# Pseudo-random factors on the ranks of a scan's weave, early splits of two inputs, and head sums by four column tiles

## The chip, the core and the metric

The kernel runs on one core of a Trainium2 chip, in one launch. The time is device microseconds of one execution on the chip; lower is better. Before the change the median of three runs was 1632.7 us (1623.32 to 1636.57).

An engine executes its own instructions strictly in the order in which they were written into its program. TensorE is called PE here (PEld is its loading of stationary operands), VectorE DVE, ScalarE ACT, GpSimd POOL, SyncE SP. SP and POOL issue the transfers between the core's memory and DRAM.

## The reference, cut to what matters

Two requests, each of 512 tokens by 1024 channels, go through two layers with shared weights. Layer 0 is a bidirectional RWKV-7 mixer, layer 1 a neighbourhood attention on a grid. All is float32.

```python
x_prev = jnp.pad(xn[:, :-1], ((0, 0), (1, 0), (0, 0)))
x_next = jnp.pad(xn[:, 1:], ((0, 0), (0, 1), (0, 0)))
xx = 0.5 * (x_prev + x_next) - xn
lerp = lambda j: xn + xx * mu[j]
r = heads(lerp(0) @ w_r).astype(f32)
k = heads(lerp(1) @ w_k).astype(f32)
v = heads(lerp(2) @ w_v).astype(f32)
z = xn @ w_z
kk = k * k_k.astype(f32).reshape(N_HEADS, HEAD_DIM)
kk = kk / jnp.maximum(jnp.sqrt(jnp.sum(kk * kk, axis=-1, keepdims=True)), 1e-12)
...
def step(s, inp):                       # one token of the WKV scan
    r_t, w_t, k_t, v_t, a_t, b_t = inp
    sa = jnp.einsum('bhvk,bhk->bhv', s, a_t)
    s = s * w_t[:, :, None, :] + sa[..., None] * b_t[:, :, None, :] + v_t[..., None] * k_t[:, :, None, :]
    return s, jnp.einsum('bhvk,bhk->bhv', s, r_t)
...
ys.append(_wkv7_scan(r, decay, k_d, v, -kk, kk * a, reverse=(d == 1)))   # d = 0, 1; 16 heads of 64
...
out = y.reshape(bsz, t, D_INNER).astype(xn.dtype) * jax.nn.silu(z)
return out @ w_o
```

Layer 1 multiplies by `w_in` (q, k, v and gate), attends to an 8 by 16 window, gates, and multiplies by `w_ao`. RMS norms stand around both layers.

## The kernel before, in words

**Tiles.** Activations lie with channels on the 128 partitions: eight tiles of 128 by 512 (k = 0 to 7). A product by a weight column (128 output channels) takes eight k-steps. For precision each operand is split into a rounded float32r half and a rest: ACT casts the high half, DVE subtracts (L403 and L404, `halves`; in the scan L806 and L808 for weights, L832 and L834 for inputs). A k-step is three matmuls of 128x512: high by high, high by low, low by high (L454 to L456 in `gemm`, L887 to L889 in the scan). Weight halves live in four pairs of buffers (`whi`, `wlo`, NW = 4), two pairs to a column. Input halves live in 18 buffers (`act`).

**Stage 1, the prelude** (`run`, `prelude`, `columns`, `column`). PE multiplies request 0 by `w_z` (8 columns), by the first LoRA factors, then by `w_k` (8 columns). Beside it DVE and ACT normalise both requests, form the shifted sums `xx`, and mix them with the inputs by a learned factor (`lerp`: ACT scales, L675, DVE multiplies and adds, L676). The mixed inputs of request 1, and that for v of request 0, go to DRAM by way of four `ls` buffers (`mixed`, 32 of them). Those for k and r of request 0 are mixed into `xr` and split into `act` buffers by `shifted`: the ones for k where the z columns end, the ones for r after the k columns have been written. In this stage a list scheduler sets each engine's order, from priorities in the order of the code and its own estimates of durations.

**Head sums.** After each k column `column` copies it out (L717), squares it (L726, tile `tmp`), sums the squares over the 64 channels of each of its two heads by one plain float32 matmul with a stationary operand of two columns (L730, profiled as two instructions), copies the 2x512 result (L733) and stores it to DRAM. When the eighth is there, 16 rows are loaded, a square root (L744) and a reciprocal (L747) are taken, and the result `rn` is stored. `prep`, below, loads it.

**Stage 2, the scan** (`scan_phase`, `weave`). Here a planner of the kernel writes the order of PE, DVE and ACT. Work is cut into threads. Each names the engine of its next piece and when that may start by the planner's clock; of those that may start now, all that are not for PE come ahead of those for PE, and then the lowest rank wins. Ranks are: the 64 scan steps 0; the factors of the next step 0.5 and 1 (`alone`, `near`, `outer`); `preps` 1.5; posts of a product column 2; `merges` 2.4; splits of inputs 2.5; splits of weights 3 or 9; `finish` 4; `inverse` 5; the products 9. A split that the products will soon lack gets 1.2. The products (`flow`) are the remaining columns of both requests' layer 0 (r, v, k, z, the output), and most of layer 1's input columns for request 0: 84 columns, 672 k-steps. Where the planner finds nothing to do on PE for 300 ns and its clock window not full, it writes a filler matmul into spare room (L1730) which computes nothing that is used.

The scan runs in 8 groups of 8 steps (2 requests by 4 sets of 4 heads). Before a group stand `prep` (L977 to L1070: decays, keys and so on, with a round trip of `ab` through DRAM), an elimination on DVE (`elimination`, a chain of 60 instructions L1096 and L1098 between two transposes, L1089 and L1109) and `merges`.

**Stage 3, the rest** (`rest`): what remains of layer 1 for request 0, attention, and request 1's output and layer 1, again in the list scheduler's order.

## Time and profile before

| | |
|---|---|
| median of 3 runs | 1632.7 us (1623.32, 1632.70, 1636.57) |
| the profiled execution | 1627.51 us, of which its span is 1625.7 us |
| busy in the span | PE 1533.0 us (94%), DVE 1219.6 (75%), ACT 974.4 (60%), POOL 199.4 (12%) |
| mean granted TensorE clock | 0.978 |
| chain that ended last | PE 71%, DVE 10%, DMA 8%, ACT 5%, issue 5% |
| prelude | PE from 8.8 us to 154.4 us |
| scan, first to last step | 253.1 us to 1101 us |
| last product of the scan stage | 1143 us |

The span is what the profiled execution took from its first instruction to its last. A row of the timeline has the start, the time that it covers, engine, line, operation, output tile from input tiles, shape and count, and, in brackets, how long the engine sat idle before it and what ended that. Matmuls overlap: a 128x512 matmul is shown as about 390 ns, while its neighbours start some 230 ns apart, and it is the distance of the starts that counts. In a table of windows the granted clock (PEclk) is a share of full speed.

### The profile page before, as it was taken

The page shows a single profiled execution, that of the slowest core. Times are in us where ns is not written, and L with a number is a line of the kernel's source. Part 1 is how long each engine was busy: PE and PEld are TensorE (multiplying, and loading weights), DVE is VectorE, ACT ScalarE, POOL GpSimd, SP SyncE. Part 2 cuts the span into 40 slices and gives each one's busy share as a digit, 9 for nine tenths or more (in the row PEclk, how much of TensorE's full clock was granted, in tenths as well). Part 3 has the DMA queues.
Part 4 walks back from the last instruction along what each step waited for, and adds up shares of the span by engine and source line. Part 5 has one row for each costly group of instructions (what it writes and reads, how often), then busy time and mean ns, then how long its engine had stood idle before and what let it go on. Part 6 is the DMA issues. An engine that isn't in the chain of part 4 may idle for free.

```text
span 1625.7 us, 46321 instructions
## 1 busy us (share of the span) xinstructions
PE 1533.0 (94%) x18700; PEld 1177.7 (72%) x18700; DVE 1219.6 (75%) x2714; ACT 974.4 (60%) x1933; POOL 199.4 (12%) x368
## 2 busy tenths in 40 slices
PE   7989998899989998988999999999999999999998
PEld 6856776666667776766777777777777788777776
DVE  8986587689878788885899999656667585664664
ACT  6567565756647456656676655544567665464562
POOL 0001123301111012122000011000110002110110
PEclk9989999999999999998999999999999999999999
DMA  6447687766676867678776785565766356655553
GB/s 242 158 164 260 217 277 233 261 203 224 196 235 202 261 233 225 207 234 261 234 261 232 253 259 170 160 200 196 258 213 184 115 151 225 225 187 192 170 168 110
DMA packets 183542, 343.61 MB, mean 211 GB/s; under 512 B 25856, under 2 KB 58752, under 8 KB 183328
## 3 DMA queue, kind: packets, MB, share of 16 engines
q1 hardware_dynamic: 158144, 256.75, 49.4%
q0 software_dynamic: 25184, 83.90, 14.7%
q8 instruction: 147, 2.41, 0.6%
q14 instruction: 67, 0.55, 0.1%
HBM read 230.33 MB, written 107.09 MB: 208 GB/s over the span
## 4 chain that ended last, share of the span: by engine, by line
PE 71%; DVE 10%; DMA 8%; ACT 5%; issue 5%; SPq 0%; DVEq 0%; POOL 0%; ACTq 0%; POOLq 0%
PE pm L887 8%; PE pg L456 7%; PE pm L888 6%; PE pm L889 6%; PE pg L454 6%; PE pg L455 6%; PE pf L1199 3%; PE sc L1538 2%; DMA dab<-ab 2%; PE po L1571 2%; PE pt L1556 2%; PE us L1318 2%; PE zy L1271 2%; PE us L1298 2%; PE zy L1322 2%
## 5 line engine op out<-in xcount | busy, mean ns | idle before, releaser
L887 PE MATMUL pm<-act,whi 128*128 128x512 f32 x672 | 297.0, 442 | 2.4 <-ACT NA L1141 1.2
L888 PE MATMUL pm<-act,whi 128*128 128x512 f32 x672 | 269.4, 401 | 7.1 <-DVE act L834 7.0
L889 PE MATMUL pm<-act,wlo 128*128 128x512 f32 x672 | 268.5, 400 | 6.3 <-DVE wlo L808 6.3
L887 PEld LDWEIGHTS pm<-act,whi 128*128 128x128 f32 x672 | 128.9, 192 | 45.4 <-issue 12.9
L454 PE MATMUL pg<-act,whi 128*128 128x512 f32 x384 | 157.7, 411 | 0.0
L889 PEld LDWEIGHTS pm<-act,wlo 128*128 128x128 f32 x672 | 128.9, 192 | 37.0 <-DVE wlo L808 8.3
L888 PEld LDWEIGHTS pm<-act,whi 128*128 128x128 f32 x672 | 129.5, 193 | 33.6 <-DVE act L834 12.1
L456 PE MATMUL pg<-act,wlo 128*128 128x512 f32 x384 | 153.0, 398 | 0.0
L455 PE MATMUL pg<-act,whi 128*128 128x512 f32 x384 | 152.5, 398 | 0.0
L404 DVE TENSOR_TENSOR wlo<-raw,whi 128x512 fp32r<-128x512 f32 x148 | 101.7, 689 | 67.7 <-ACT whi L403 62.2
L403 ACT CAST whi<-raw 128x512 fp32r<-128x512 f32 x148 | 91.2, 617 | 94.2 <-PE pg L455 64.0
L808 DVE TENSOR_TENSOR wlo<-raw,whi 128x512 fp32r<-128x512 f32 x168 | 114.7, 684 | 30.2 <-ACT whi L806 30.1
L806 ACT CAST whi<-raw 128x512 fp32r<-128x512 f32 x168 | 103.7, 620 | 42.0 <-PE pm L888 34.8
L456 PEld LDWEIGHTS pg<-act,wlo 128*128 128x128 f32 x384 | 72.3, 188 | 18.0 <-issue 4.0
L1098 DVE TENSOR_TENSOR N<-etmp,N 128x30 f32<-128x30 f32 (+14 forms) x240 | 78.8, 328 | 4.6
L1096 DVE TENSOR_TENSOR etmp<-N 128x30 f32<-128x30 f32 (+14 forms) x240 | 78.7, 328 | 4.6
L455 PEld LDWEIGHTS pg<-act,whi 128*128 128x128 f32 x384 | 72.5, 189 | 13.1 <-issue 1.3
L454 PEld LDWEIGHTS pg<-act,whi 128*128 128x128 f32 x384 | 72.3, 189 | 12.1 <-issue 0.7
L1552 ACT ACTIVATE sb<-sb,mx 128x256 f32<-128x256 f32 x128 | 64.2, 503 | 23.7 <-DVE mx L1551 22.9
L1199 PE MATMUL pf<-cab 64*64 64x128 f32 (+1 forms) x2048 | 67.6, 268 | 5.6 <-issue 5.2
L1310 ACT COPY X<-us 64x256 f32<-64x256 f32 x128 | 46.9, 366 | 34.4 <-PE zy L1177 32.8
L1222 DVE TENSOR_TENSOR AK<-zy,cc 128x256 f32<-128x256 f32 x63 | 26.6, 423 | 51.7 <-PE zy L1177 49.5
(393 smaller groups left out, 3552.1 us busy)
## 6 DMA issues: line engine op xcount, KB each, us to landing
dab<-ab POOLq DMA_DIRECT2D x32, 1024.0 KB, 7.2
cab<-dab SPq DMA_DIRECT2D x64, 512.0 KB, 4.5
raw<-in_w_in_dram SPq DMA_DIRECT2D x128, 256.0 KB, 3.9
bias<-in_rpb_dram SPq DMA_DIRECT2D x32, 384.0 KB, 4.7
raw<-in_w_z_dram SPq DMA_DIRECT2D x32, 256.0 KB, 4.3
raw<-in_w_k_dram SPq DMA_DIRECT2D x32, 256.0 KB, 2.4
raw<-in_w_r_dram SPq DMA_DIRECT2D x32, 256.0 KB, 4.4
k<-dk SPq DMA_DIRECT2D x32, 256.0 KB, 4.0
```

The lines of the kernel that those rows point to most:

```text
L403: self.nc.scalar.copy(hi, src)
L404: (eng or self.nc.vector).tensor_tensor(lo, src, hi.bitcast(F32), op=ALU.subtract)
L454: nc.tensor.matmul(ps, hi, x[k][0], start=(k == 0), stop=False)
L455: nc.tensor.matmul(ps, hi, x[k][1], start=False, stop=False)
L456: self.mm = nc.tensor.matmul(ps, lo, x[k][0], start=False, stop=(k == KT - 1))
L806: nc.scalar.copy(hi, raw[h])
L808: nc.vector.tensor_tensor(lo, raw.pop(h), hi.bitcast(F32), op=ALU.subtract)
L887: nc.tensor.matmul(ps, hi[:, at], xh, start=(k == 0), stop=False)
L888: nc.tensor.matmul(ps, hi[:, at], xl, start=False, stop=False)
L889: nc.tensor.matmul(ps, lo[:, at], xh, start=False, stop=(k == KT - 1))
L1098: vt.tensor_tensor(N[:, q + 1:, :q], tv, N[:, q + 1:, :q], op=ALU.add)
L1199: end = nc.tensor.matmul(st.f[half(a), h, 0, d, g] if st.last else st.f[half(a), h, :, d, g], ab[half(h), d, g, 2 * e[d] + 1 - a], rt if s ...
```

## The change

It has six parts.

1. **Factors on ranks.** In `weave` a rank is multiplied by `1 + 0.4 u`, with u drawn evenly from -1 to 1 anew for each candidate each time. The generator is seeded anew whenever the number of finished steps passes a multiple of four, from a table of 17 seeds. Five of them are 0, and there ranks stay as they were (segments 1, 7 and 14 to 16).
2. **k inputs early.** `prelude(0)` mixes and splits request 0's inputs for k right after the LoRA matmuls have been written, into the 16 buffers `lw` that held LoRA weights.
3. **r inputs early.** A generator `ahead`, advanced at a quarter of the rate of the k columns, mixes and splits the inputs for r, and loads and splits both halves of the first `w_r` column. These hold two of the four weight buffers until the scan's first product.
4. **Head sums by four tiles.** The matmul of 2x512 becomes four, each of 32 stationary columns (16 copies of either head's selector, with the value 0.5, which the scale 2.0 in the square root makes good) on 128 tokens, to partitions 0, 32, 64 and 96. The copy is 128x128 instead of 2x512, and eight of its rows go to DRAM. The planner's cost for a 128x32 tile is changed with it.
5. **Head sums later.** A k column's sum is not written with its column but after the fourth k-step of the next. The last one becomes a thread of the weave (`tail`, rank 0).
6. **Order in the prelude.** Request 1's norm waits 14 more turns (`HOLD`); request 0's mixed v goes from the end of `prelude(0)` into `prelude(1)`, each with a wait on the latest matmul written.

```diff
-        elif ts == (128, 128):
+        elif ts in ((128, 128), (128, 32)):
             c = max(1.73 * n + 1, 100.0)
...
+    RATE, HOLD = 0.25, 14
+    SEEDS, SIG, SEG = (653160, 0, 317010, 943442, 878710, 392232, 801855, 0, 390308, 625245, 854555, 218764, 664198, 404737, 0, 0, 0), 0.4, 4
...
-        self.ident, self.bones, self.ssel = c("ident", 128), c("bones", 128), c("ssel", 2)
+        self.ident, self.bones, self.ssel = c("ident", 128), c("bones", 128), self.cc[:, CC["bones"] + 48:CC["bones"] + 80]
...
+        for _ in range(s * self.HOLD):
+            yield
         rstd = self.rstd(acc, (lambda: self.mm) if s else None)
...
         if s:
             for k in range(KT):
+                self.mixed(0, "v", 2, k, self.mm)
+                yield
+            for k in range(KT):
                 for kind, j in (("k", 1), ("r", 0), ("v", 2)):
...
+        for k in range(KT):
+            hi, lo = (self.t("lw", (P, 4, 2, 64), 16, F32R, self.lp).rearrange("p k q c -> p (k q c)") for _ in range(2))
+            t = self.t("xr", bufs=self.NXR)
+            self.lerp(t, xn[k], xx[k], 8 + k)
+            self.xk.append(self.halves(t, lo, hi))
+            yield
...
+    def ahead(self):
+
+        xn, xx = self.shift[0]
         for k in range(KT):
-            mixed("v", 2, k)
+            lo, hi = self.pair()
+            t = self.t("xr", bufs=self.NXR)
+            self.lerp(t, xn[k], xx[k], k)
+            self.xr.append(self.halves(t, hi, lo))
+            yield
+        for raw in self.raws(self.a["w_r"][0]):
+            hi, lo = (self.t(tag, (P, self.WP), self.NW, F32R) for tag in ("whi", "wlo"))
+            self.wr.append(self.halves(raw, lo, hi))
             yield
...
-            ss = self.p("pm", (2, T))
-            nc.tensor.matmul(ss, self.ssel, sq, start=True, stop=True)
+            ss = self.p("pm", (P, P))
+            for j in range(4):
+                nc.tensor.matmul(ss[32 * j:32 * j + 32], self.ssel, sq[:, j * P:(j + 1) * P], start=True, stop=True)
             yield "A"
-            row = self.tmp((2, T))
+            row = self.tmp((P, P))
             act.copy(row, ss)
...
-            self.load(sp["ss", s][2 * p:2 * p + 2], row)
+            self.load(sp["ss", s][2 * p:2 * p + 2].rearrange("a (j t) -> j a t", j=4), row[0:P:16])
...
-                act.activation(rn, rn, AF.Sqrt)
+                act.activation(rn, rn, AF.Sqrt, scale=2.0)
...
     def columns(self, s, kind, x, ps=range(NP)):
+        self.tail = None
         for p in ps:
             w = self.first.pop() if self.first else self.weight(self.a["w_" + kind][p])
-            ps = yield from self.gemm(w, x, self.gt)
-            for _ in self.column(s, kind, p, ps):
-                pass
+            gemm, n = self.gemm(w, x, self.gt), 0
+            while True:
...
+                n += 1
+                if n == 4 and self.tail:
+                    run(self.tail[1])
+                    self.tail = None
+                yield
+            end = self.column(s, kind, p, out)
+            if kind == "k":
+                for _ in range(3):
+                    at = next(end)
+                self.tail = at, end
+            else:
+                run(end)
             yield
...
+            if did["steps"] // self.SEG != part:
+                part = did["steps"] // self.SEG
+                dice = Random(self.SEEDS[part])
...
-                    key = (t.eng == "P", t.rank())
+                    key = (t.eng == "P", t.rank() * (1.0 + self.SIG * dice.uniform(-1.0, 1.0) if self.SEEDS[part] else 1.0))
...
+        def tail():
+            (eng, gate, needs), end = self.tail
+            yield eng, gate, lambda c: max(needs(c), 2500.0)
+            yield from end
...
-        run(self.columns(0, "k", self.shifted(0, 1)), (a, 1))
+        run(self.columns(0, "k", self.xk), (a, 1), (self.ahead(), self.RATE))
         run(a)
-        self.xr = self.shifted(0, 0)
```

What this does to the order is shown at three places. A row has the line, the operation, the output tile from the input tiles with their buffer numbers, and the shape. The rows of the kernel after have its own line numbers: L457 to L459 are L454 to L456 of before, L485 is L482, L499 is L496, L759 is L730, L937 to L939 are L887 to L889, L1784 is L1730, L1184 is L1134.

PE at request 1's norm, before: `acc` is the sum of request 1's squares, `pm` the norm's banks, `zy_979` the first k column.

```order
L456 MATMUL zy_979<-act_936,wlo_972 128x512
L454 MATMUL zy_979<-act_943,whi_975 128x512
L482 MATMUL pm_865<-ones,acc_782 128x1 x4
L455 MATMUL zy_979<-act_942,whi_975 128x512
L456 MATMUL zy_979<-act_943,wlo_976 128x512
```

PE at the same norm, after: `zy_1064` is the third k column, `zy_1144` the fourth, `tmp_951` and `tmp_1042` the squares of the first and second.

```order
L459 MATMUL zy_1064<-lw_706,wlo_1061 128x512
L485 MATMUL pm_976<-ones,acc_798 128x1 x4
L499 MATMUL pm_989<-tmp_984,ones 128x128
L759 MATMUL pm_1006<-tmp_951,cc 32x128 x4
L499 MATMUL pm_989<-tmp_984,ones 128x128 x3
L759 MATMUL pm_1082<-tmp_1042,cc 32x128 x4
L457 MATMUL zy_1144<-lw_616,whi_1136 128x512
```

The norm has moved from the middle of the first k column to behind the third. Its second half (L499) follows its first (L485) directly, where eight rows of products stood between the two before, and two head sums stand there too.

PE where the prelude ends and the products of the scan begin, before: `zy_1471` is the last k column, `zy_1594` the filler's bank, `pm_1618` the first r column.

```order
L456 MATMUL zy_1471<-act_964,wlo_1468 128x512
L730 MATMUL pm_1454<-tmp_1452,cc 2x512
L730 MATMUL pm_1502<-tmp_1500,cc 2x512
L1730 MATMUL zy_1594<-cc 128x256 x6
L887 MATMUL pm_1618<-act_1518,whi_1609 128x512
```

PE at the same place, after: `zy_1545` is the last k column, `pm_1622` the first r column, `tmp_1526` the squares of the seventh k column.

```order
L459 MATMUL zy_1545<-lw_706,wlo_1542 128x512
L759 MATMUL pm_1565<-tmp_1526,cc 32x128 x4
L937 MATMUL pm_1622<-act_928,whi_1291 128x512
L938 MATMUL pm_1622<-act_929,whi_1291 128x512
L939 MATMUL pm_1622<-act_928,wlo_1292 128x512
L937 MATMUL pm_1622<-act_953,whi_1291 128x512
L938 MATMUL pm_1622<-act_954,whi_1291 128x512
L939 MATMUL pm_1622<-act_953,wlo_1292 128x512
```

The sum that is left there is the seventh. The last one (`pm_1640`) has moved from ahead of the first r column to behind its twelfth matmul, and the six fillers are gone.

ACT in the last k columns, before: `ls` are mixed inputs on their way to DRAM, `whi` weight halves, `xr` and `act` the inputs for r, of which the last four are made after the last column's square (L726).

```order
L726 ACTIVATE tmp_1500<-zy_1471,cv 128x512
L403 CAST act_1546<-xr_1542 128x512
L675 ACTIVATE xr_1556<-xn_131,dv 128x512
L403 CAST act_1553<-xr_1549 128x512
L733 COPY tmp_1504<-pm_1502 2x512
```

ACT at the same place, after: `pm_1640` is the last column's head sum, L754 is L726, L762 is L733, L701 is L675, L856 is L806.

```order
L754 ACTIVATE tmp_1589<-zy_1545,cv 128x512
L701 ACTIVATE ls_1391<-xn_788,dv 128x512
L701 ACTIVATE ls_1399<-xn_788,dv 128x512
L762 COPY tmp_1654<-pm_1640 128x128
L856 CAST whi_1666<-raw_1635 128x512
```

The inputs for r are gone from there, and the mixed inputs of request 1 have moved behind: the last 14 of the 32 now stand behind the last k column's square, among the splits for the r columns, where none stood before.

In the whole weave, the rows of L1730 add up to 62 fillers before and those of L1784 to 42 after. The rows from the first attention scores to the end of the program are nearly the same in both.

33 lines of the change are left out of this document (24 added, 9 removed).

## The prediction

> **What bounds the kernel now.** I read the page first, then a table of windows by stage, then PE's timeline where it stops, then the groups for prices. The page's busy times:
>
> ```profile
> PE 1533.0 (94%) x18700; PEld 1177.7 (72%) x18700; DVE 1219.6 (75%) x2714; ACT 974.4 (60%) x1933; POOL 199.4 (12%) x368
> ```
>
> PE is busy nearly all the time, so what can be won is PE's idle time, its slow clock, fillers, and matmuls that become cheaper. The windows by stage (columns: window, length, busy us and count of PE, PEld, DVE, ACT, POOL, granted clock, DMA share, GB/s) say where these are. The cuts are PE's first wait in the first k column, the first r product, the first scan step, the fourth group's start, the last step and the last product:
>
> ```profile
> 0.00:82.00 82.00, 72.94 (x315) 59.19 (x316) 72.23 (x155) 52.65 (x87) 1.53 (x40) 1.00 0.58 200
> 82.00:154.00 72.00, 61.91 (x225) 41.50 (x224) 57.42 (x94) 54.73 (x96) 3.67 (x3) 0.88 0.59 210
> 154.00:253.00 99.00, 91.55 (x736) 71.47 (x734) 68.60 (x123) 56.85 (x109) 20.57 (x35) 0.98 0.74 247
> 253.00:605.00 352.00, 324.73 (x5736) 240.96 (x5737) 282.69 (x553) 213.67 (x419) 52.48 (x88) 0.96 0.70 224
> 605.00:1101.00 496.00, 464.42 (x8762) 356.61 (x8765) 406.30 (x797) 302.85 (x574) 66.35 (x107) 0.98 0.69 225
> 1101.00:1143.00 42.00, 42.00 (x248) 33.25 (x239) 25.67 (x54) 20.21 (x36) 3.24 (x6) 1.00 0.67 231
> 1143.00:1626.00 483.00, 475.46 (x2699) 374.67 (x2697) 306.68 (x945) 273.46 (x614) 51.54 (x89) 1.00 0.56 181
> ```
>
> From 1101 us on PE is busy at full clock, and nothing of the change is there: whatever is won before shifts all of it. The k columns (82 to 154 us) are the worst stage: 10 us idle and a clock of 0.88. In the scan PE is idle for 27 us and then 32 us, and the clock, 4% and 2% short, costs some 14 us and 10 us more. There DVE is busy 80% and 82%. PE's timeline in the k columns names the waits:
>
> ```profile
> 83.57 0.51 PE L454 MATMUL zy<-act,whi 128*128 128x512 f32 x1 [1.00 <-ACT act L403]
> 87.14 1.84 PE L482 MATMUL pm<-ones,acc 128*128 128x1 f32 x8 [3.06 <-DVE acc L469]
> 102.78 1.87 PE L730 MATMUL pm<-tmp,cc 128*2 128x512 f32 x2 [2.44 <-ACT tmp L726]
> 148.39 1.86 PE L730 MATMUL pm<-tmp,cc 128*2 128x512 f32 x2 [3.48 <-ACT tmp L726]
> 150.18 4.55 PE L1730 MATMUL zy<-cc 128*128 128x256 f32 x12
> 154.38 0.59 PE L887 MATMUL pm<-act,whi 128*128 128x512 f32 x1
> ```
>
> PE waits for the first split input, for the norm's sum, twice for a square, and then six fillers (two instructions each) pass until the first r inputs are split. The clock falls behind each of these:
>
> ```profile
> 80.00:90.00 10.00, 5.94 (x24) 4.68 (x23) 10.00 (x18) 6.57 (x12) 0.00 (x0) 0.77 0.31 105
> 90.00:100.00 10.00, 9.89 (x42) 7.58 (x40) 8.93 (x19) 9.91 (x17) 0.00 (x0) 0.89 0.18 66
> 100.00:110.00 10.00, 7.55 (x22) 3.65 (x21) 10.00 (x18) 5.25 (x10) 0.00 (x0) 0.83 0.66 251
> 140.00:150.00 10.00, 6.52 (x22) 3.13 (x20) 7.85 (x12) 9.98 (x19) 1.85 (x2) 0.84 0.60 225
> 150.00:160.00 10.00, 10.00 (x37) 8.10 (x37) 5.67 (x12) 6.30 (x13) 0.00 (x0) 0.82 0.67 186
> ```
>
> **The change part by part.** *Early k and r inputs, later sums, the moved norm.* By the order all four waits lose their cause: k inputs are split before the k columns, the norm stands two columns later, most sums wait for squares that are half a column old or more, and r inputs and the first r weights are ready when the last k column ends. Idle time removed: 1.00 + 3.06 + 2.44 + 3.48 = 10.0 us. The fillers are gone too: 154.38 - 150.18 = 4.2 us. The slow clock in the five slices is 10 x (0.23 + 0.11 + 0.17 + 0.16 + 0.18) = 8.5 us; 14 of those 50 us were idle or fillers, so the share on products is about 6 us.
>
> Against it stand new waits. Behind the third k column the norm's two halves follow each other directly, with ACT and DVE work between them, and at the fifth column a sum stands three rows behind the end of its own column, on a square that ACT reaches only after two mixed inputs that wait for stores. The nearest row for either is the 2.44 us above, so 4.9 us; at best 0, at worst 3.48 each and a third one, 10. The row of slice 100 to 110 shows that a wait of 2.44 us already took the clock to 0.83 there, so I add 1.7 us once. By the Trainium skill (TensorE: Matmul & The Clock Gate, "What's actually happening") the clock falls after an idle window of about 3.4 us. This trace differs: 2.44 us sufficed. By the page's figure the 1.7 us would not come.
>
> *The price of a head sum.* In an undisturbed place a sum costs what it pushes its neighbours apart:
>
> ```profile
> 136.96 0.39 PE L456 MATMUL zy<-act,wlo 128*128 128x512 f32 x1
> 137.28 1.02 PE L730 MATMUL pm<-tmp,cc 128*2 128x512 f32 x2
> 138.23 0.50 PE L454 MATMUL zy<-act,whi 128*128 128x512 f32 x1
> ...
> 229.45 0.39 PE L889 MATMUL pm<-act,wlo 128*128 128x512 f32 x1
> 229.68 1.03 PE L764 MATMUL pm<-cc,tmp 128*128 128x128 f32 x8
> 230.52 0.50 PE L887 MATMUL pm<-act,whi 128*128 128x512 f32 x1
> ...
> 1157.24 1.09 PE L1571 MATMUL po<-pts,vtok 128*64 128x128 f32 x16
> 1158.27 1.13 PE L1538 MATMUL sc<-k,q 64*128 64x256 f32 x6
> ```
>
> The distance is 1.27 us, less the 0.23 us of a product's own: 1.04 us. Eight full-width instructions of 128 take 0.84 us (229.68 to 230.52), as many columns as a sum's two of 512, so 0.2 us of a sum is the change of tile form. Four tiles are again eight instructions of 128. Two column tiles that alternate take 1.03 / 16 = 0.064 us each, against 0.84 / 8 = 0.105: they run side by side. By that row eight instructions take 0.51 us, were all four side by side 0.21; were they one after the other, 0.84. With the 0.2 us a sum then costs 0.4 to 1.04 us. I take 0.55, between the first two: 0.5 us less. Eight in the prelude give 4 us (0 to 5), eight in the scan 4 us.
>
> The Trainium skill has a rule against this (TensorEngine Tiling (Array Packing), "Key Properties"): a change of tiling mode drains the engine. The trace bears a price out, the 0.2 us, but the sum of before pays it as well, so it does not speak between the two.
>
> *The copy of a sum* is a quarter as long. ACT spends 0.571 us on it now:
>
> ```profile
> L733 ACT COPY tmp<-pm 2x512 f32<-2x512 f32 x16 | 9.1, 571 | 14.5 <-PE pm L730 14.4
> ```
>
> Some 0.35 us by 16 is 6 us of ACT work, at 60% busy: hidden by PE's products, counted at nothing. A store of eight short rows instead of two long ones also has nobody waiting but at the last sum.
>
> *What of the prelude's lead survives.* The first r product comes earlier by 10.0 + 4.2 + 6 + 4 - 4.9 - 1.7 = 17.6 us, near 137 us. But the scan begins with a chain, head sums to `rn` to `prep`, and its last sum has moved from ahead of the first r column into it:
>
> ```profile
> 165.50 1.46 PE L1730 MATMUL zy<-cc 128*128 128x256 f32 x6
> 166.86 0.50 PE L977 MATMUL pm<-h,w2h 128*128 128x512 f32 x1
> ...
> 253.07 0.46 PE L1277 MATMUL zy<-V,AK 64*64 64x64 f32 x16 [1.01 <-DVE AK L1222]
> ```
>
> The first `prep` matmul stood 12.5 us behind the first r product. The last sum was done 4.2 us ahead of that product, and now comes 12 matmuls, 2.8 us, behind it: `prep` stands about 19.5 us behind, at 156 to 157. Beside it lie 14 mixed inputs that used to be over:
>
> ```profile
> L675 ACT ACTIVATE ls<-xn,dv 128x512 f32<-128x512 f32 x32 | 21.9, 715 | 6.1 <-DVE xn L563 2.3 <-DMA dlk<-ls 2.3 <-DMA dlr<-ls 0.7
> L676 DVE SCALAR_TENSOR_TENSOR ls<-xx,dv,ls 128x512 f32<-128x512 f32 x32 | 23.0, 751 | 7.1 <-ACT ls L675 7.0
> ```
>
> 14 x 0.715 = 10 us of ACT and 14 x 0.751 = 10.5 us of DVE, spread over these 19.5 us, in which DVE was busy two thirds of the time: they just fit, and this is what could eat the lead. `prep` and the first step (253.07) then come about 10.5 us earlier; the other 7 us are nine k-steps done ahead of `prep`, products that no longer lie there when PE has gaps to fill. Half of them, 3 us, I count as won. SP's queue gets the same stores in another order; nothing is added to it.
>
> *Factors on ranks.* The scan steps have rank 0, which no factor changes. What is shuffled is who gets DVE and ACT among splits, `preps`, `merges`, `outer`, posts and the elimination. No row shows a shuffled order, so I take the order's own trace of idle time, the fillers. Three of them (six instructions) took 166.86 - 165.50 = 1.36 us, 0.45 us each. They fall from 62 to 42, six of these 20 being those counted above; 14 x 0.45 = 6.3 us. I take 5, since PE may idle where the planner sees none. From below zero (a chain lengthened, the last rival) to three times that.
>
> *The sum:* 10.5 + 3 + 4 + 5 = 22.5 us, and 2 us more for slow clock that goes with the scan's idle time (a twelfth of the 24 us above): 24.5. The profiled execution took 1627.5 us, so 1603. The median of the runs lay 5.2 us above it; I allow a fifth of that: **1604 us**, own range 1594 to 1614.
>
> **The rivals.** *The lead is lost at the first step.* The mixed inputs, each waiting for one of four buffers to be stored, hold up ACT's queue, with the weight splits and `w2h` (L964) behind them. For it: all 14 stand ahead of `prep` on ACT and DVE. Against it: by their busy time they fit. Then only 4 + 5 us stay: 1627.5 - 9 = 1618.5, or 1620 against the runs. Chance 0.17.
>
> *More is won.* The new waits do not come (24.2 us at the first r product), all of it carries, the scan's idle time shrinks by twice what the fillers say (10) and a third of its slow clock (8) goes: with the 4 of the sums 46 us, 1582; with half of what this has over the forecast, 1592. For it: 59 us of idle time and 24 of slow clock lie there. Against it: DVE at 80% sets the pace between groups, and loses no work. Chance 0.21.
>
> *Four tiles are one after the other.* The sums then cost about what they did: 8 us less is won, 1612, still faster. Chance 0.05.
>
> *A shuffled DVE lengthens the chain to a group, and the kernel is slower.* Its place is DVE between two groups, where the elimination's 60 dependent instructions are mixed with splits:
>
> ```profile
> L808 DVE TENSOR_TENSOR wlo<-raw,whi 128x512 fp32r<-128x512 f32 x168 | 114.7, 684 | 30.2 <-ACT whi L806 30.1
> L1098 DVE TENSOR_TENSOR N<-etmp,N 128x30 f32<-128x30 f32 (+14 forms) x240 | 78.8, 328 | 4.6
> ```
>
> Each split more between its two transposes delays the group by up to 0.684 us. Seven groups wait so; with n splits more in each the loss is 4.8 n, against 24.5 won: even at n = 5, slower by over 1% from n = 9, at n = 11 about 1632. That is with the lead kept; with the lead lost it takes n = 6, and n = 8 gives 1656. For it: elimination has rank 5, splits 3, and factors from 0.6 to 1.4 let them pass. Against it: in the order the other rows between the transposes are 673 in all before and 669 after, fewer in three of the eight, more in five. Chance 0.07, at 1655.
>
> **How the numbers follow.** The forecast has 0.50. About 1%, 16 us, is what a measurement of this kernel can tell from no change: faster lies below 1616, slower above 1649. Faster: 0.50 + 0.21 + 0.05, and 0.02 of the lost lead's range: 0.78. Slower: 0.07. Within 1%: 0.15. The range goes from 1586, most of the second rival, to 1624, the lost lead with its spread; left out are the last rival and the best of the second.
>
> **What would show it.** In the profile after: the first r product (L937) near 137 us with no filler ahead of it, and a PEclk of 1.00 in most slices from 80 to 140; two waits of 1 to 3 us left, at L499 and at the fifth L759; four L759 (eight instructions) in 0.3 to 0.6 us; the first L1027 near 157 and the first step near 242; 84 filler instructions instead of 124; the first L1538 some 24 us earlier, and the time from there the same. A first step at 250 or later makes the lost lead right; steps that start late group by group make the last rival right; a first step near 230 and less idle time in every group the second.

## The result, and the profile after

| | before | after |
|---|---|---|
| median of 4 runs | 1631.7 us (1623.3 to 1636.6) | 1607.9 us (1604.5 to 1608.1) |
| ratio after to before | | 0.9867, 95% interval 0.9829 to 0.9904 |
| the profiled execution, its span | 1627.5 us, 1625.7 us | 1608.0 us, 1606.2 us |
| PE's first r product | 154.4 us | 138.5 us |
| first scan step | 253.0 us | 252.1 us |
| scan, first step to last | 848.0 us | 835.4 us |
| last step to the end | 524.7 us | 518.7 us |

The change makes the kernel 1.3% faster, 24 us by the medians and 19.5 us by the two spans. The forecast was 1604 us. The spans split as 0.9 us before the first step, 12.6 us in the scan and 6.0 us behind it (the cuts lie within 0.4 us of the events). The busy times of the page after:

```profile
PE 1512.5 (94%) x18756; PEld 1170.9 (73%) x18756; DVE 1221.5 (76%) x2714; ACT 968.3 (60%) x1931; POOL 199.3 (12%) x368
```

PE was busy 20.5 us less (1533.0 before), and idle as long as before: 1606.2 - 1512.5 = 93.7 us against 92.7. The windows by stage, with the cuts at the events at which those of before were cut (k columns, first r product, first step, fourth group, last step, last product; columns as in the prediction):

```profile
0.00:82.00 82.00, 72.94 (x314) 59.25 (x315) 73.95 (x158) 54.28 (x92) 1.53 (x40) 1.00 0.51 174
82.00:138.90 56.90, 53.04 (x258) 40.18 (x257) 46.91 (x77) 39.99 (x73) 0.00 (x0) 0.91 0.69 236
138.90:252.10 113.20, 92.84 (x668) 71.89 (x666) 73.10 (x125) 59.66 (x114) 20.58 (x33) 0.92 0.71 241
252.10:604.00 351.90, 325.29 (x5899) 245.41 (x5899) 299.23 (x590) 225.92 (x445) 56.54 (x95) 0.99 0.73 235
604.00:1087.50 483.50, 457.01 (x8713) 350.36 (x8715) 397.90 (x774) 297.01 (x563) 66.17 (x107) 0.98 0.69 226
1087.50:1123.50 36.00, 36.00 (x220) 28.72 (x210) 20.61 (x32) 16.10 (x25) 3.05 (x6) 1.00 0.64 204
1123.50:1606.20 482.70, 475.42 (x2706) 375.07 (x2705) 309.78 (x964) 275.38 (x622) 51.48 (x89) 1.00 0.57 185
```

The k columns are 15 us shorter (56.9 us against 72.0). The stretch behind them, up to the first step, is 14 us longer (113.2 against 99.0), and PE is idle there for 20.4 us where it was idle for 7.5: the lead is won in the one and lost in the other. The clock is lower there too: summed over slices of 10 us, it falls short of full speed by 8.5 us, against 1.7 before.

PE's timeline shows all three waits that are left in the k columns (in brackets the idle time):

```profile
99.44 0.69 PE L499 MATMUL pm<-tmp,ones 128*128 128x128 f32 x2 [1.94 <-DVE tmp L495]
102.69 0.66 PE L759 MATMUL pm<-tmp,cc 128*32 128x128 f32 x8 [0.40 <-ACT tmp L754]
119.20 0.43 PE L759 MATMUL pm<-tmp,cc 128*32 128x128 f32 x8 [1.52 <-ACT tmp L754]
```

They are the two that the prediction named and a third of 0.4 us, 3.9 us in all where it counted 4.9. Where the lead then goes is seen on SP's queue, on DVE and on PE, each from its own timeline:

```profile
150.57 0.48 SPq L359 DMA_DIRECT2D drn<-tmp  x1
...
159.84 0.32 SPq L353 DMA_DIRECT2D dlv<-ls  x1
160.26 1.16 SPq L359 DMA_DIRECT2D rb<-drn  x2
161.47 0.58 SPq L359 DMA_DIRECT2D k<-dk  x1
...
165.26 0.75 DVE L1012 SCALAR_TENSOR_TENSOR rb<-k,cv,rb 128x512 f32<-128x512 f32 x1 [3.49 <-DMA k<-dk]
165.93 0.69 DVE L858 TENSOR_TENSOR wlo<-raw,whi 128x512 fp32r<-128x512 f32 x1
...
166.67 0.79 PE L939 MATMUL pm<-act,wlo 128*128 128x512 f32 x1 [10.50 <-DVE wlo L858]
167.26 0.63 PE L1027 MATMUL pm<-h,w2h 128*128 128x512 f32 x1
...
252.24 0.46 PE L1327 MATMUL zy<-V,AK 64*64 64x64 f32 x16
```

`rn` was stored at 150.6 us, but the loads of `rb` and `k` for the first `prep` start only at 160.3 and 161.5, behind the last store of a mixed input. DVE stands at L1012 until `k` is there, the rest of a weight column (L858) is behind it in DVE's order, and PE waits 10.5 us for that. The first `prep` matmul comes at 167.3 us (before 166.9).

Behind the last step lie fewer products. These are the windows of the product line alone (columns: window, length, busy us and count of PE and PEld, clock, DMA share, GB/s), after and then before:

```profile
252.10:1087.50 835.40, 236.24 (x530) 100.91 (x530) 0.98 0.71 230
1087.50:1606.20 518.70, 19.25 (x46) 8.63 (x46) 1.00 0.57 186
```

```profile
253.00:1101.00 848.00, 235.88 (x523) 100.70 (x523) 0.97 0.70 225
1101.00:1625.70 524.70, 22.01 (x53) 9.96 (x53) 1.00 0.57 185
```

Seven k-steps more were done inside the scan. At 0.68 us each (three products 0.23 us apart) that is 4.8 of the 6.0 us behind it. The fillers fell too, by 12.7 us of PE (34.2 us in 124 instructions before), of which 4.5 us are the six that stood ahead of the first r product:

```profile
L1784 PE MATMUL zy<-cc 128*128 128x256 f32 x84 | 21.5, 382 | 0.6 <-ACT Z L1333 0.6
```

So the time did not come out of the prelude, where I had put most of it. It came out of the scan: fewer slots without work in the planned order, and more products done under it. PE's idle time in the scan fell from 58.9 to 53.1 us, and the time by which the scan's clock falls short of full speed, again by slices of 10 us, from 24 to 17 us. The experiments ask two things: who holds the lead up, and which of the six parts made the scan shorter.

### The profile page after: what moved, and what is told of

It is laid out like the page before. It is cut to its first block, busy times and chain, and to the rows that moved or that the text cites. A ratio compares the mean times of both kernels' runs of the same rounds, so it can differ in the third digit from the quotient of the medians.

```text
span 1606.2 us, 46435 instructions
## 1 busy us (share of the span) xinstructions
PE 1512.5 (94%) x18756; PEld 1170.9 (73%) x18756; DVE 1221.5 (76%) x2714; ACT 968.3 (60%) x1931; POOL 199.3 (12%) x368
## 4 chain that ended last, share of the span: by engine, by line
PE 68%; DVE 11%; DMA 9%; ACT 6%; issue 5%; SPq 0%; POOL 0%; DVEq 0%; ACTq 0%; POOLq 0%
PE pm L937 7%; PE pg L459 7%; PE pg L457 6%; PE pg L458 6%; PE pm L939 5%; PE pm L938 5%; PE pf L1249 3%; PE sc L1588 2%; PE po L1621 2%; PE pt L1606 2%; PE us L1368 2%; DMA cab<-dab 2%; DMA dab<-ab 2%; DVE ab L1071 2%; PE zy L457 2%
## 5 line engine op out<-in xcount | busy, mean ns | idle before, releaser
L937 PE MATMUL pm<-act,whi 128*128 128x512 f32 x672 | 296.0, 440 | 5.3 <-ACT vs L796 2.8
L939 PE MATMUL pm<-act,wlo 128*128 128x512 f32 x672 | 268.7, 400 | 12.8 <-DVE wlo L858 12.8
L937 PEld LDWEIGHTS pm<-act,whi 128*128 128x128 f32 x672 | 128.6, 191 | 46.7 <-issue 10.8
L939 PEld LDWEIGHTS pm<-act,wlo 128*128 128x128 f32 x672 | 128.8, 192 | 43.7 <-DVE wlo L858 14.9
L457 PE MATMUL pg<-act,whi 128*128 128x512 f32 x384 | 156.5, 408 | 0.0
L459 PE MATMUL pg<-act,wlo 128*128 128x512 f32 x384 | 152.9, 398 | 0.0
L858 DVE TENSOR_TENSOR wlo<-raw,whi 128x512 fp32r<-128x512 f32 x166 | 113.3, 684 | 29.5 <-ACT whi L856 28.3
L856 ACT CAST whi<-raw 128x512 fp32r<-128x512 f32 x166 | 102.2, 619 | 32.9 <-PE pm L938 25.2
L459 PEld LDWEIGHTS pg<-act,wlo 128*128 128x128 f32 x384 | 72.1, 188 | 18.2 <-issue 4.0
L458 PEld LDWEIGHTS pg<-act,whi 128*128 128x128 f32 x384 | 72.4, 189 | 13.1 <-issue 1.0
L457 PEld LDWEIGHTS pg<-act,whi 128*128 128x128 f32 x384 | 72.2, 188 | 12.5 <-issue 0.7
L1031 ACT ACTIVATE th<-pm,dv 128x512 f32<-128x512 f32 x64 | 43.9, 686 | 30.0 <-PE pm L1028 29.5
```

The source lines that it names most:

```text
L457: nc.tensor.matmul(ps, hi, x[k][0], start=(k == 0), stop=False)
L458: nc.tensor.matmul(ps, hi, x[k][1], start=False, stop=False)
L459: self.mm = nc.tensor.matmul(ps, lo, x[k][0], start=False, stop=(k == KT - 1))
L856: nc.scalar.copy(hi, raw[h])
L858: nc.vector.tensor_tensor(lo, raw.pop(h), hi.bitcast(F32), op=ALU.subtract)
L937: nc.tensor.matmul(ps, hi[:, at], xh, start=(k == 0), stop=False)
```

## The experiments

Each run was timed against the kernel before on the same chip. "Pairs" are the planned fillers, two instructions each.

| run | what differs | pairs | ratio to before, 95% interval | first step | scan | behind it |
|---|---|---|---|---|---|---|
| before | | 62 | 1 | 253.0 | 848.0 | 524.7 |
| after | all six parts | 42 | 0.9867 (0.9829 to 0.9904) | 252.1 | 835.4 | 518.7 |
| `pool_stores` | after, stores of mixed inputs on POOL | 42 | 0.9902 (0.9866 to 0.9939) | 254.7 | 834.4 | 519.0 |
| `loads_apart` | and `prep`'s buffers elsewhere | 42 | 0.9855 (0.9818 to 0.9892) | 250.6 | 829.4 | 518.6 |
| `loads_apart_wide` | and more buffers for mixed inputs | 42 | 0.9878 (0.9838 to 0.9918) | 247.5 | 833.9 | 518.9 |
| `no_factors` | after, all seeds 0 | 89 | 1.0300 (1.0245 to 1.0355) | 252.7 | 884.7 | 539.4 |
| `factors_only` | before, and part 1 | 59 | 0.9958 (0.9931 to 0.9984) | 256.9 | 840.6 | 517.4 |
| `other_seeds` | after, another table | 52 | 1.0084 (1.0055 to 1.0114) | 250.6 | 870.0 | 521.1 |
| `median_seeds` | after, a third table | 67 | 1.0075 (1.0046 to 1.0103) | 250.0 | 859.6 | 520.9 |
| `early_only` | before, and parts 2, 3, 5, 6 | 89 | 1.0114 (1.0081 to 1.0147) | 252.8 | 858.2 | 526.4 |
| `sums_only` | before, and part 4 | 87 | 1.0166 (1.0116 to 1.0217) | 252.5 | 851.4 | 543.2 |
| `sums_same_order` | the same, scan's order of before | 62 | 0.9996 (0.9972 to 1.0019) | 248.8 | 844.3 | 524.3 |
| `old_sum_own_order` | after without part 4 | 85 | 1.0202 (1.0162 to 1.0242) | 253.3 | 859.4 | 545.6 |
| `old_sum_same_order` | the same, scan's order of after | 42 | 0.9900 (0.9868 to 0.9932) | 252.8 | 835.3 | 518.9 |

The last three columns are us of one profiled execution each, good to some 0.2 us. The chips differ a little, so runs are compared by their ratios. Five runs have the change's order in the scan (`after`, `pool_stores`, `loads_apart`, `loads_apart_wide`, `old_sum_same_order`), and their scans take 829.4 to 835.4 us; two have the order of before (`before`, `sums_same_order`), and theirs take 848.0 and 844.3.

### Who holds the lead up

First theory: SP's queue, in which the stores stand ahead of the loads. The stores were moved to POOL's queue.

```diff
-        return self.nc.gpsimd if kind == "hid" or self.away and kind not in ("y", "x1", "h") else self.nc.sync
+        return self.nc.gpsimd if kind in ("hid", "lk", "lr", "lv") or self.away and kind not in ("y", "x1", "h") else self.nc.sync
```

> The kernel after, with the stores of the 32 mixed inputs (ls to DRAM) issued by POOL instead of SP; PE's, DVE's and ACT's order in the weave is word for word that of after. Theory: prep's loads (rb, k, r) stood behind these stores on SP's queue (rb was issued at 160.26 us, 9.7 us after rn's store), so the lead of 15.5 us at the first r product was gone at the first step. Then the first prep matmul comes at 155 to 160 us instead of 166.8, the 10.5 us idle of PE before it falls to 3 or less, the first step comes near 243 instead of 252, and the whole is 7 to 10 us faster than after, near 1599. Rival: the lead is eaten by the 14 mixed inputs' own work on ACT and DVE; then the first prep stays at 165 to 167, the first step at 250 or later, and the time is that of after within 3 us.

Measured: 1609.3 us, no gain over the change. PE's wait at L939 is 12.3 us, the first `prep` matmul comes at 169.3 and the first step at 254.7. The time and the first step are those of the rival. Three timelines of this run, SP's queue, ACT and DVE:

```profile
149.80 0.33 SPq L359 DMA_DIRECT2D drn<-tmp  x1
150.35 0.50 SPq L359 DMA_DIRECT2D raw<-in_w_r_dram  x1
161.30 1.16 SPq L359 DMA_DIRECT2D rb<-drn  x2
...
159.68 1.55 ACT L701 ACTIVATE ls<-xn,dv 128x512 f32<-128x512 f32 x2 [0.32 <-DMA dlk<-ls]
...
160.44 1.58 DVE L704 SCALAR_TENSOR_TENSOR ls<-xx,dv,ls 128x512 f32<-128x512 f32 x2 [0.30 <-ACT ls L701]
```

SP's queue is empty from 150.9 to 161.3, and the load of `rb` still starts late. It starts when ACT's last two mixed inputs are done (159.68 + 1.55 = 161.23). The buffers of the scan's stage lie over those of the prelude, and those of `rb`, so the new theory, over inputs that ACT still reads. The theory that the queue alone holds the loads falls. In the next run the two pools of the scan's stage changed places, which leaves PE's order in the scan as it was; the stores stay on POOL, so whether the queue would hold the loads as well is not tested:

```diff
-        self.front = self.pool(mid, "right")
-        self.pp = self.pool(prep, "right")
+        self.pp = self.pool(mid, "right")
+        self.front = self.pool(prep, "right")
```

> The change whole, with the scan's prep buffers laid where no mixed input lies (the two pools of the scan swapped), and the mixed inputs' stores on POOL's queue. With the stores on POOL alone, the loads of rb, k and r still started at 161.3 us, just after ACT's last mixed input (159.7 us, two of 1.55 us), although SP's queue was empty from 150.9 us: their buffers, not the queue, held them. Theory: now they start behind the store of rn at about 150, the first prep matmul (L1027) comes near 158 to 160 instead of 166.8, the wait of 10.5 us at L939 shrinks to under 5, and the first step starts near 245 instead of 252. What of that reaches the end: if the scan passes a lead on (its planned order is the same, 42 pairs of fillers), 1600 to 1603. Rival: another wait of the same size takes its place before the first step (operands of the products, or the weights), and the time stays 1606 to 1610.

SP's queue, ACT and PE in this run:

```profile
149.01 0.33 SPq L359 DMA_DIRECT2D drn<-tmp  x1
149.55 0.33 SPq L359 DMA_DIRECT2D raw<-in_w_r_dram  x1
151.22 1.17 SPq L359 DMA_DIRECT2D rb<-drn  x2
...
158.22 0.72 ACT L701 ACTIVATE ls<-xn,dv 128x512 f32<-128x512 f32 x1 [2.33 <-DMA dlr<-ls]
159.72 0.72 ACT L701 ACTIVATE ls<-xn,dv 128x512 f32<-128x512 f32 x1 [0.78 <-DVE ls L704]
160.94 1.34 ACT L701 ACTIVATE ls<-xn,dv 128x512 f32<-128x512 f32 x2 [0.50 <-DMA dlk<-ls]
162.19 0.99 ACT L1811 COPY cab<-cc 64x64 f32<-64x64 f32 x4
163.20 0.62 ACT L1014 CAST w2h<-tmp 128x512 fp32r<-128x512 f32 x1
...
164.70 0.80 PE L939 MATMUL pm<-act,wlo 128*128 128x512 f32 x1 [10.22 <-DVE wlo L858]
```

The load of `rb` now starts at 151.2, and PE still waits 10.2 us. The second holder stands at the same place in time: the mixed inputs, waiting for one of four buffers to be stored, with `w2h` behind them on ACT. That is the mechanism of the prediction's first rival. It had been covered by the first holder. The rival expectation, a wait of the same size in its place, holds; the time, 1605.2 us, lies between the ranges of the two. The third run gives the last nine mixed inputs 16 buffers that are free by then:

```diff
-        t = self.t("ls", (P, T), 4, F32, self.lp)
+        if s and k >= 5:
+            t = self.t("lw", (P, 4, 2, 64), 16, F32R, self.lp).rearrange("p k q c -> p (k q c)").bitcast(F32)
+        else:
+            t = self.t("ls", (P, T), 4, F32, self.lp)
```

> As the run with the prep's buffers apart, and the last nine mixed inputs (k from 5 on) written into the sixteen buffers of the k inputs, which are read by then, instead of the ring of four. With the buffers apart the loads of rb and k started at 151.2 and 152.4 us, but ACT's queue still held the weights' cast: its mixed inputs waited for the stores of the ring (2.3, 1.3 and 1.0 us at a time) until 162.2, the copy w2h came at 163.2 and the cast behind it at 164.2, and PE waited 10.2 us at L939. Theory: the ring was the second holder; now w2h comes before 158, the wait at L939 is under 5 us, the first step starts at 243 to 247, and the time is 1596 to 1602. Rival: a third holder at about the same time (the loads of the next weights, which start only behind the casts), first step at 249 to 252 and 1602 to 1608.

ACT, DVE and PE in this run:

```profile
157.33 0.62 ACT L1017 CAST w2h<-tmp 128x512 fp32r<-128x512 f32 x1
...
162.44 0.75 DVE L1015 SCALAR_TENSOR_TENSOR rb<-k,cv,rb 128x512 f32<-128x512 f32 x1 [5.74 <-DMA k<-dk]
...
163.85 0.50 PE L942 MATMUL pm<-act,wlo 128*128 128x512 f32 x1 [4.41 <-DVE wlo L861]
...
247.47 0.46 PE L1330 MATMUL zy<-V,AK 64*64 64x64 f32 x16
```

`w2h` comes 5.9 us sooner, PE's wait is 4.4 us instead of 10.2, and the first step starts at 247.5, 4.8 us ahead of the change. Two holders are shown, but they are not all: the first `prep` matmul moved from 167.3 us to 165.3 and 164.2 only, and the prediction had 156 to 157. In the last run SP issues the load of `k` at 156.0, 3.6 us later than in the run before it, and DVE stands 5.7 us for it; PE has waited 3.7 us for the square of the last head sum before that. So a third holder took over, of another kind than the rival named; it was not removed. The first step (243 to 247 expected) and the time, 1603.2 us (1596 to 1602), lie just outside the theory's ranges. None of the three runs can be told from the change by its time. Whether such a lead reaches the end is not shown: this run's span is 5.9 us shorter than that of the change, but its ratio, 0.9878, lies within the interval of the change's 0.9867. Four to six runs of a kernel don't resolve 5 us here, and one profiled execution does so still less (below, `sums_same_order`).

### Which part made the scan shorter

The theory was that the factors give most of it, through planned slots without work, and that the other parts give a little each. First the change without factors, then the factors without the rest.

```diff
-    SEEDS, SIG, SEG = (653160, 0, 317010, 943442, 878710, 392232, 801855, 0, 390308, 625245, 854555, 218764, 664198, 404737, 0, 0, 0), 0.4, 4
+    SEEDS, SIG, SEG = (0,) * 17, 0.4, 4
```

> The kernel after with all seeds 0: ranks without factors, all other parts kept. The planner then writes 89 fillers (after 42, before 62). Theory: what after won between the first and the last step (12.7 us) came from the shuffled order alone; without it the time is 12 to 20 us above after, 1620 to 1628, and the first step stays near 252. Rival: it came from the cheaper head sums and the work already done ahead; then the time stays within 5 us of after, 1603 to 1613, though the order has more fillers.

```diff
+    SEEDS, SIG, SEG = (653160, 0, 317010, 943442, 878710, 392232, 801855, 0, 390308, 625245, 854555, 218764, 664198, 404737, 0, 0, 0), 0.4, 4
...
-                    key = (t.eng == "P", t.rank())
+                    key = (t.eng == "P", t.rank() * (1.0 + self.SIG * dice.uniform(-1.0, 1.0) if self.SEEDS[part] else 1.0))
```

> The kernel before with the factors on ranks alone, by the same 17 seeds. The planner writes 59 fillers (before 62). Theory: a table of seeds is good only for the program it goes with; on another program it is one shuffled order among many, so the time is that of before within 8 us either way. Rival: shuffling as such is good (or these seeds are), and the time is 12 us or more below before, 1620 or less.

> The kernel before with the head sums by four column tiles alone (with the planner's cost for them). Theory: a sum costs some 0.6 us less on PE, 16 of them 9 to 10 us, half of that in the prelude; but the planner's order turns out another one with 87 fillers instead of 62 (25 x 0.45 = 11 us), so the time is that of before within 6 us, and the first step comes 2 to 5 us earlier. Rival: fillers only show idle time that is there anyway; then the time is 8 to 10 us below before, near 1622.

Measured: 1676.0, 1619.9 and 1650.3 us. Parts 2 to 6 without factors are 50 us slower than the kernel before. Part 4 alone, which saves PE time at each sum, is 25 us slower. The first and the last lie outside what theory and rival had allowed. The factors alone, by the seeds of the change, are 0.4% faster, as the theory had it. The parts are not terms of a sum: each of them alters what the planner books, and so the whole order behind it.

The next pair holds the arithmetic fixed and changes the order alone. Both runs are the change with the old head sum (the reverse of the diff of part 4). In one the planner books it as it is, which gives another order from the third group on. In the other it is booked as the four tiles would be:

```diff
+        if f32 and not tr and ts == (128, 32) and n == 512 and tp[1] == 0 and not self.four:
+            self.four = True
+            for j in range(4):
+                i4 = SimpleNamespace(is_transpose=False, tile_size=ts, tile_position=(tp[0], 32 * j))
+                r = self.matmul(i4, ins, 128, t if j == 0 else max(t, self.t["P"]))
+            self.four = False
+            return r
```

> The same arithmetic as in the run beside it (one f32 matmul of 2x512 for a head sum), but booked by the planner as it is, so that the scan gets another order from its third group on: 85 pairs of fillers instead of 42. Theory: the scan's planned order is what decides; by the runs so far a pair more costs between 0.86 us (the head sums alone against before: 25 pairs, 21 us) and 1.5 us (no factors against the change: 47 pairs, 71 us), so 43 pairs give 37 to 65 us on top of the run beside it, 1645 to 1680. Rival: the order matters little and the head sums alone made the difference in the earlier runs: within 5 us of the run beside it.

> The change whole but with the head sum as one f32 matmul of 2x512, as before; the planner books it as if it were four tiles, so that every engine's order in the scan is that of the change (42 pairs of fillers). This is the price of the head sum by itself. PE was busy 1.02 us with the old sum and 0.43 us with the four tiles, 16 sums in all: theory, 5 to 9 us slower than the change, 1613 to 1617. Rival: a sum's time is hidden beside its wait for ACT (L759 waits 3.0 us in all), so nothing, 1606 to 1610.

Measured: 1660.3 us (1659.9 to 1663.3) in its own order, 1612.0 (1608.8 to 1621.3) in that of the change. The same work takes 48 us more in the other order (the fillers aside, the instructions are the same). The expectation, 37 to 65 us more, holds. The product line's windows and the filler's group, first in the order of the change, then in its own:

```profile
252.80:1088.10 835.30, 233.88 (x530) 99.59 (x530) 0.99 0.71 230
1088.10:1607.00 518.90, 19.27 (x46) 8.65 (x46) 1.00 0.57 186
...
L1794 PE MATMUL zy<-cc 128*128 128x256 f32 x84 | 21.6, 382 | 0.6 <-ACT Z L1343 0.6
```

```profile
253.30:1112.70 859.40, 221.66 (x491) 94.17 (x491) 0.97 0.67 219
1112.70:1658.30 545.60, 34.47 (x85) 15.98 (x85) 1.00 0.56 184
...
L1783 PE MATMUL zy<-cc 128*128 128x256 f32 x170 | 44.8, 397 | 0.6 <-ACT Z L1332 0.6
```

In the other order 39 k-steps fewer are done by the last step (491 against 530), and the stretch behind it is 26.7 us longer: 39 x 0.68 = 26.5. The scan itself is 24.1 us longer as well. The fillers take 23.2 us more, no more than the products that have left the scan, so it is not they that lengthen it. PE is idle there 13.1 us longer (69.8 us against 56.7), and by slices of 10 us its clock falls short of full speed by 29 us, against 7. So a product that is not done in a gap of the scan comes at the end, a filler takes its place, and in this order more waits and a slower clock come on top. The clock is lower in each of its four runs (0.972 to 0.976, against 0.977 to 0.988 in the six of the other); whether it falls for the waits alone is not shown.

Then the table of seeds itself. Of 22 further tables (drawn blindly, in the same segments) the planned order has 52 to 80 pairs of fillers, the median 67. The one with the fewest and one from the middle were run.

> The change whole with other seeds in the same segments: 52 pairs of fillers instead of 42. Theory (the planned gaps tell the time, whatever the table): 10 pairs at 0.76 to 1.5 us, 1616 to 1623. Rival (this table was one in many, and any other is as bad as none, whatever its gaps): 1650 to 1676, near the run without factors.

> The change whole with other seeds, taken from the middle of the planned orders: of 22 further tables the scan got 52 to 80 pairs of fillers, the median 67, and this one has 67; no factors 89, the change 42. Theory: without factors the order is a bad one, and any shuffle mends part of it, the table of the change most: 1640 to 1660, slower than before and faster than without factors (1676). Rival: only a picked table helps, an ordinary one is as good as none: 1668 to 1685. Second rival: any shuffle gives what the change gives, 1600 to 1620.

Measured: 1643.2 and 1637.3 us. Both are slower than before (1.0084 and 1.0075), and faster than without factors. An ordinary table mends most of what the other parts spoil (1.0300 without factors), the second a little more of it than expected; the table of the change is better than both by some 34 us. But the counts don't tell the time: 52 pairs are not faster than 67, and ten pairs more than the change cost 35 us, not the 8 to 15 expected. That theory falls, and so does its rival, which had such a table near the run without factors. The busy times of the run with 52 pairs:

```profile
PE 1524.3 (93%) x18776; PEld 1181.0 (72%) x18776; DVE 1222.8 (74%) x2714; ACT 968.8 (59%) x1931; POOL 199.3 (12%) x368
```

Its PE is idle for 1641.7 - 1524.3 = 117.4 us against 93.7: two thirds of its loss by the spans, 35.5 us, are waits that no filler fills. The rest is PE's busy time, 11.8 us more: 6.8 us of fillers (28.3 against 21.5), and a lower clock (0.971 against 0.979). The early parts alone were the last of these:

> Of the change only the early parts: k and r inputs split early, the k columns' ends later, the second sequence's norm held back; the head sum and all ranks are those of before. The scan's order comes out with 89 pairs of fillers (before 62, the change 42). Theory: the prelude's lead is gone at the first prep, as in the change, and the scan's order decides: 1650 to 1680. Rival: the 15 us by which the first r product comes earlier are a gain on their own, whatever the order: 1612 to 1625.

Measured: 1644.1 us, 1.1% slower than before, below the range of the theory and far from the rival's. Its first step is at 252.8 us, so its prelude gave nothing either. It has as many pairs as `no_factors`, 89, and is some 30 us faster by the ratios.

### What a head sum is worth

The four tiles were put into the kernel before, with the planner booking the old matmul, so that PE's order in the scan is that of before, row for row.

```diff
+        if ins[0].bass_ap.tensor.name in self.sum:
+            rows, n = (0, 2), 512
...
+        if f32 and not tr and ts == (128, 32):
+            self.sum.add([x for x in i.outs if hasattr(x, "bass_ap")][0].bass_ap.tensor.name)
+            if tp[1]:
+                return self.whole
+            n = 512
```

> The kernel before, with its head sums by four tiles, but booked by the planner as the one matmul of 2x512, so that PE's order in the scan is that of before row for row (62 pairs of fillers). In the change a sum cost 0.45 us in an undisturbed place (two neighbours 0.68 us apart, less a product's 0.23), before 1.04; 16 sums, so 9.4 us of PE. Theory (the saving counts where PE is the bound): 5 to 10 us faster than before, ratio 0.994 to 0.997. Rival (a sum's time lies in a wait anyway): the same as before within 2 us. The four tiles by themselves with the planner's new price ran at 1.0166; if it is the order alone that cost that, this run is not slower than before by either.

Measured: 1626.9 us against 1628.2, ratio 0.9996 (0.9972 to 1.0019): at most 4.6 us of the 9.4 us are won, and perhaps none: the rival's range, not the theory's. The group of the sums in this run, busy time and the idle time before them:

```profile
L740 PE MATMUL pm<-tmp,cc 128*32 128x128 f32 x128 | 7.0, 293 | 8.6 <-ACT tmp L735 8.6
```

The wait for ACT's square is 8.6 us (8.4 before, by the views of waits): a shorter sum does not shorten the wait ahead of it. In the change the same replacement was worth 0.9900 - 0.9867, some 5 us, and those two intervals overlap. What is shown is that it is worth less than PE's saving in the one kernel; in the other it may be worth anything from nothing to all of it. That part 4 alone was 25 us slower is the order: with the same four tiles in the order of before nothing is lost.

This run's profiled execution has a span 8.3 us shorter than that of before, and its 12 runs don't differ from 17 of before. Differences of a few us between two spans, those of the three runs on the lead included, are no finding by themselves.

## Why the prediction was right, and where it was not

The time came out within 4 us of the forecast, by other terms than mine. Of 10.5 us that I had ahead of the first step 0.9 came, and behind it 18.6 us where I had 14. Two errors of opposite sign met: that the sum is so near is partly luck.

**The k columns: right.** The four waits, 10.0 us, are gone; the two new ones that I had named came, and a third of 0.4 us, 3.9 us in all (4.9 forecast); the fillers between the last k column and the first r product are gone. The slices of 10 us from 80 to 140 after:

```profile
80.00:90.00 10.00, 10.00 (x44) 8.03 (x43) 9.94 (x17) 9.70 (x18) 0.00 (x0) 1.00 0.38 134
90.00:100.00 10.00, 8.06 (x39) 6.52 (x37) 8.88 (x19) 5.06 (x8) 0.00 (x0) 0.98 0.50 155
100.00:110.00 10.00, 9.60 (x49) 6.90 (x48) 7.43 (x12) 7.35 (x14) 0.00 (x0) 0.68 0.55 211
110.00:120.00 10.00, 8.48 (x55) 5.97 (x55) 10.00 (x17) 6.03 (x12) 0.00 (x0) 1.00 0.68 236
120.00:130.00 10.00, 10.00 (x38) 7.97 (x37) 5.13 (x8) 5.68 (x10) 0.00 (x0) 0.83 1.00 333
130.00:140.00 10.00, 10.00 (x55) 7.32 (x55) 7.54 (x12) 9.22 (x18) 0.00 (x0) 1.00 0.97 326
```

The slow clock is 10 x (0.02 + 0.32 + 0.17) = 5.1 us, against 8.5 in the five slices of before; I had added 1.7 us only, and a clock of 1.00 in most of these slices; three of the six have it. The first r product came at 138.5 us, 15.9 us earlier, where I had 17.6. On the clock the Trainium skill (TensorE: Matmul & The Clock Gate, "What's actually happening") asks for an idle window of some 3.4 us; here a wait of 1.94 us (with 0.40 us more behind it) was followed by a slice at 0.68, and one of 1.52 us by a slice at 0.83. As in the trace of before, the measured rows decide against the rule as a threshold for idle time.

**The price of a sum: right; its worth: mis-sized.** In an undisturbed place after:

```profile
109.65 0.40 PE L457 MATMUL zy<-lw,whi 128*128 128x512 f32 x1
109.98 0.43 PE L759 MATMUL pm<-tmp,cc 128*32 128x128 f32 x8
110.33 0.50 PE L458 MATMUL zy<-lw,whi 128*128 128x512 f32 x1
```

The neighbours stand 0.68 us apart, less 0.23 is 0.45 us (0.55 forecast, 1.04 before). The term of 8 us counted nearly all of that as time of the kernel. The runs show less than 4.6 us of the whole 9.4 in the kernel before, and about 5 in the change, with an uncertainty as large.

**What of the prelude's lead survives: this step failed.** I had 10.5 us at the first `prep` and at the first step, and 3 more for nine k-steps done ahead. At the first `prep` there was nothing (167.3 us against 166.9), at the first step 0.9 us, and as many k-steps done as before, 96. The last product of the scan stage came 19.5 us earlier (1143.0 to 1123.5), what follows took as long as before, and the first attention score, for which I had named some 24 us, came 12.8 us earlier. My reckoning asked whether ACT and DVE had the time for the 14 mixed inputs that moved behind the k columns. They had: with buffers enough (`loads_apart_wide`) both are through with them by 156.4 us. What I had not looked at is what `prep`'s loads and casts stand behind: the loads wait for buffers that the mixed inputs still use, and `w2h` stands behind mixed inputs that wait for stores. The first rival named the second of these and a first step at 250 us or later as its mark; it is right on what happened, with a first holder that I had not seen, and a third behind the two. Its time, 1620, was wrong, since it left the scan only 9 us.

**The factors: mis-sized, and mis-named.** I had 5 us, with a bound of three times that. In the scan and behind it 18.6 us were won. The eight sums there save PE 8 x 0.59 = 4.7 us at most, so about 14 us or more are the order's. The scans say the same: 835.3 us in the order of the change with the old sums, 844.3 in the order of before with the new ones. And the order is not the factors' alone: the same factors in the kernel before gave 6 us by the medians on their chip (0.9958), the other parts without factors lost 3%. The number belongs to one table in one program.

**Slow clock: mis-sized.** I had 2 us for the scan. By slices of 10 us the shortfall there went from 24 us to 17. Between the first r product and the first step, where I had nothing, it grew from 1.7 us to 8.5, beside PE's new waits.

**The rival on the slower side** got 0.07, and the change didn't take that way. But with two tables out of two that were not the change's own, the kernel was slower than before. That the table decides the sign is something I had not weighed: I took the count of fillers as a measure of the order, and between one table and another it is none. Why the change's order leaves 24 us less idle time than one with ten pairs more stays open; no single wait carries it. One number of that rival is a slip: by 24.5 - 4.8 n, eleven splits more in each group give 1656 us, and 1632 belongs to six.

## What to carry to other kernels

When an edit feeds a planner, price it twice: once with the order held fixed (let the planner book the old cost), once with the order that it gets. Here the same work differed by 48 us through the order alone, and an edit that saves PE 9 us came out 25 us slower. A lead that was won ahead of a barrier was worth nothing here. Before counting one, follow each thing that the barrier's loads wait for, their buffers' last readers and their place in each queue: removing one holder only showed the next.

## What the runs showed of the hardware

Four column tiles of 128x32 in turn, eight instructions on 128 columns, cost PE 0.45 us between full-width products, against 1.04 us for two instructions of 512 columns with a stationary operand of two: eight full-width ones of 128 take 0.84, so the tiles run side by side. TensorE's granted clock was 0.83 and 0.68 in slices that follow waits of only 1.5 and 1.9 us.
